# Stick-breaking attention step: ScalarE reads the accumulators, GpSimd adds, and transposes share a PSUM ring with the scores

## The chip, the core and the metric

One core of a Trainium2 chip runs the program. The metric is device time in microseconds (us), the median of several executions. Before the change it is 1325.29 us (three runs, 1322.95 to 1325.57).

## The reference, cut to what matters

One layer is computed for a prompt of 2048 tokens and for 64 tokens of a running stream, in float32:

```
h = rms_norm(x) * g_norm;  z = h @ w_in          # 1024 -> 3072 columns
q_sb, k_sb, v_sb, g_sb, u_pool, g_pool, q_xa, g_xa = split(z)
# A) stick-breaking attention, 8 heads of 64, strictly causal
s = q k^T / 8;  w[q,k] = sigmoid(s[q,k]) * prod_{k<k'<q} sigmoid(-s[q,k']);  o_sb = w v
# B) causal pooling with windows 2/4/8/16;  C) cross-attention into 256 memory tokens
mixed = concat(o_sb * silu(g_sb), o_pool * silu(g_pool), o_xa * silu(g_xa))
y = rms_norm(x + mixed @ w_out) * g_final
```

The change touches the prompt's stick-breaking attention and the output rows (`x + mixed @ w_out` and the last norm) that run beside it. The kernel writes the attention with running products: c[q,k] is the product of sigmoid(-s) from key k to the query, and o = v + sum over k of c[q,k] * (v[k-1] - v[k]). So a score needs one sigmoid and one multiplying scan, and `dv` holds the differences of the values. A projection in near-float32 precision is three matmuls of rounded parts (high x high, high x low, low x high).

## The kernel before, in words

Until about 700 us the kernel normalises x, projects it (L441 to L443), does pooling, cross-attention and the running stream's 64 tokens, and stores queries, keys, values and gates to DRAM. Then comes the attention of the prompt, in four blocks of 512 queries (`s`), each for four pairs of heads (`p`). For each of these, blocks of 512 keys run from the diagonal (`j == s`) down to 0. This is `Stream.attention`, and each key block is two half blocks, one call of `Stream.step` each: 80 steps, and three more that empty the pipe.

The engines' instructions run in the order written (a manual schedule), so the text of `Stream.step` is the order of each engine's queue:

- `score` (L198): 12 matmuls for two query tiles of 128, six into each of two double banks of PSUM (`z`, a ring of two).
- `weigh`: ScalarE turns a double bank into sigmoid(-z) in SBUF (L207), and VectorE runs two scans over it (L212 on the diagonal, L214 elsewhere). A scan below the diagonal starts from the last column of the scan of the key block before it.
- `turn`, three steps later: 16 transposes of 64x128 pieces (fewer on the diagonal) of one block of 128 keys into two single banks (`pt`, a ring of two, L227), which ScalarE copies to SBUF in two copies (L230). A step turns two key blocks; the second `turn` stands behind the two `score` calls of the step.
- `run`: pieces of other dense work fill TensorE, first the gates' projections, then the output rows, three matmuls each (L1119). How many per step is set by `rate`.
- `gather` (L241): the turned weights times `dv` into the single bank `av`. After the last key block of a pair of heads, VectorE adds `vt` to `av` (L252), GpSimd multiplies with the gate (L258) and stores the result to DRAM.

`Rows` is a tile of 128 output rows. `split` rounds the loaded `mixed` on ScalarE (L1098) and takes the rest on GpSimd (L1099). `piece` accumulates eight k-tiles for each half of 512 columns in one bank `acc`; after the eighth VectorE adds x (L1122) and sums squares (L1123). `finish` does the norm on VectorE (L1131 to L1135) and stores on GpSimd's queue. A half is always followed by a stop (`None`), so the next one starts in a later step. There is one bank `av` and one `acc`: who reads them sets when TensorE can write again. Twelve such tiles run beside the attention; the last four run behind it (`tail`), in the double banks `z`.

Of the kernel before, what the change touches and what calls it, by code (L numbers as in the profile page):

```python
# [8 lines left out]
F32 = mybir.dt.float32  # L9
# [4 lines left out]
ALU = mybir.AluOpType  # L14
AX = mybir.AxisListType
PSUM = bass.MemoryType.PSUM
DRAM = bass.MemoryType.DRAM

P = 128
# [5 lines left out]
KT = D // P  # L25
# [9 lines left out]
LO, HI = slice(0, 64), slice(64, P)  # L35
# [8 lines left out]
def tile_hybrid_step(  # L44
# [30 lines left out]
    V, A, G, PE = nc.vector, nc.scalar, nc.gpsimd, nc.tensor  # L75
# [20 lines left out]
    ident = edge[:, 384:]  # L96
# [79 lines left out]
    class Block:  # L176


        def __init__(self, a, j):
            self.a, self.j = a, j  # L180
            p, room = a["p"], a["room"]
            self.K = room("K").rearrange("p (a t) -> p a t", a=2)
            dma(f(self.K), k_d[p][:, j])
            self.V = f(room("V")).rearrange("p (b d) -> p b d", b=4)
            dma(self.V, dv_d[p][:, j])
            self.diag = j == a["s"]
            self.later, a["c"] = a["c"], [None] * 4
# [29 lines left out]
        def turn(self, kb):  # L217


            room = self.a["room"]  # L220
            i0 = kb if self.diag else 0
            pts = [room("pt").rearrange("p (h i q) -> p h i q", h=2, i=4) for _ in range(2)]
            for h in range(2):
                for i in range(i0, 4):
                    for rows, pt in zip((LO, HI), pts):
                        c = self.cs[i][rows, h, kb * P : kb * P + P]
                        PE.transpose(pt[:, h, i], c, ident[rows, rows])  # L227
            w = room("w").rearrange("p (h i q) -> p h i q", h=2, i=4)
            for rows, pt in zip((LO, HI), pts):
                A.copy(w[:, :, i0:, rows], pt[:, :, i0:])  # L230
            turned = w.rearrange("p h i q -> p h (i q)")
            return kb, i0, turned

        def gather(self, kb, i0, turned):

            a, j = self.a, self.j
            room, p, s = a["room"], a["p"], a["s"]
            if self.diag and kb == 0:
                a["av"] = room("av")
            for h, rows in enumerate((LO, HI)):  # L240
                PE.matmul(  # L241
                    a["av"][rows, i0 * P :], self.V[:, kb, rows], turned[:, h, i0 * P :],
                    start=(self.diag and kb == 0), stop=(j == 0 and kb == 3),
                )
            if j == 0 and kb == 0:
                cols = slice(512 * s, 512 * s + 512)
                a["vt"], a["sg"] = room("vt"), room("sg")
                dma(a["vt"], vt_d[p][:, cols])
                dma(a["sg"], sg_d[p][:, cols])
            if j == 0 and kb == 3:  # L250
                o = room("o")
                V.tensor_tensor(o, a["av"], a["vt"], ALU.add)  # L252
                if (s, p) == LAST:

                    V.tensor_tensor(o, o, a["sg"], ALU.mult)
                    last_mixed.append(o)
                else:
                    G.tensor_tensor(o, o, a["sg"], ALU.mult)  # L258
                    store(mix_d[s][:, p], o)

    class Stream:
# [3 lines left out]


        def __init__(self, more):
            self.halves, self.pieces, self.credit = [], [], 0.0
            self.rate, self.more = 0.0, more

        def step(self, block, g):
            t = len(self.halves)
            self.halves.append((block, g))
            self.credit += self.rate
            turned = []
            b, old = self.halves[t - TURN] if t >= TURN else (None, 0)
            if b is not None:
                turned.append(b.turn(2 * old))
            if block is not None:
                first, second = block.score(2 * g), block.score(2 * g + 1)  # L280
                first()
            if b is not None:
                turned.append(b.turn(2 * old + 1))
            if block is not None:
                second()
                if g == 1:
                    block.cs = block.a["c"]
            self.run(self.credit)
            for what in turned:
                b.gather(*what)  # L290
            self.credit = min(self.credit, 6.0)

        def run(self, n):

# [61 lines left out]
    hpool = ctx.enter_context(tc.tile_pool(name="hpool", bufs=1))  # L356
    wpool = ctx.enter_context(tc.tile_pool(name="wpool", bufs=2))
    ps_acc = ctx.enter_context(tc.tile_pool(name="ps_acc", bufs=2, space=PSUM))
    ps_t = ctx.enter_context(tc.tile_pool(name="ps_t", bufs=2, space=PSUM))
    last_scope = ctx.enter_context(ExitStack())  # L360
    ps_x = last_scope.enter_context(tc.tile_pool(name="ps_x", bufs=1, space=PSUM))
    ps_last = last_scope.enter_context(tc.tile_pool(name="ps_last", bufs=1, space=PSUM))

# [271 lines left out]
    for p in range(2):  # L635
        w = chunk_of(GX0 + p)
# [12 lines left out]
    for c in range(2):  # L649
        for j in range(2):  # L650
            w, rows = WINDOWS[2 * c + j], slice(64 * j, 64 * j + 64)
# [65 lines left out]
    for c in range(2):  # L717
        w = chunk_of(U0 + c)
# [15 lines left out]
        w = chunk_of(GP0 + c)  # L734
# [95 lines left out]
    for make, c0 in ((keys, K0), (values, V0)):  # L830
        for p in range(4):
            w = chunk_of(c0 + p)
# [130 lines left out]
    for p in range(4):  # L963
        w = chunk_of(Q0 + p)
# [30 lines left out]
    def cut(t, at, *sizes):  # L995
# [9 lines left out]
    ps_z = ctx.enter_context(tc.tile_pool(name="ps_z", bufs=1, space=PSUM))  # L1005
# [9 lines left out]
        "o": cut(l3, 4096, 512) + cut(ends, 0, 512),  # L1015
        "vt": cut(ends, 512, 512, 512),
        "sg": cut(ends, 1536, 512, 512),
        "z": [ps_z.tile([P, 2, 512], F32, name=f"z{i}") for i in range(2)],
        "av": [ps_acc.tile([P, 512], F32, tag="acc", name="av")],
        "acc": [ps_acc.tile([P, 512], F32, tag="acc", name="acc2")],  # L1020
    })

    def room(name):
        if name == "pt":
            return ps_t.tile([P, 512], F32, tag="pt", name="pt")
        rings[name].append(rings[name].pop(0))
        return rings[name][-1]


    wo = {}  # L1030
# [17 lines left out]
    class Rows:  # L1048
# [56 lines left out]
        def piece(self, half, c):  # L1105
            n, xt = self.n, self.xt
            cols = slice(512 * half, 512 * half + 512)
            if c == 0 and done and half == 0:
                self.z = room("z")
            if c == 0 and not done:  # L1110
                self.acc = room("acc")
            k = self.ks[c]
            out, mh, ml = self.z[:, half] if done else self.acc, self.mh[:, k], self.ml[:, k]
            wh, wl = wo_part(k, "h")[:, cols], wo_part(k, "l")[:, cols]
            passes = [(out, mh, wh), (out, ml, wh)][: 2 if n == P else 1] + [(out[:n], mh[:, :n], wl)]
            if c == 7:
                passes.reverse()
            for i, (o, m, w) in enumerate(passes):
                PE.matmul(o, m, w, start=(c == i == 0), stop=(c == 7 and i == len(passes) - 1))  # L1119
            if c == 7:  # L1120
                for i in range(0, P, n):
                    V.tensor_tensor(xt[:n, cols], out[i : i + n], xt[:n, cols], ALU.add)  # L1122
                V.scalar_tensor_tensor(  # L1123
                    wo["sq"][:n, cols], xt[:n, cols], 1.0, xt[:n, cols], ALU.mult, ALU.mult,
                    accum_out=self.total[:n, half : half + 1],
                )

        def finish(self):
            n, xt = self.n, self.xt
# [18 lines left out]
    def output_rows():  # L1148

        if len(settled) >= SETTLED:  # L1150
            follow()
        if not following:
            return []

        if not done and len(stream.halves) - following[0].born < 2:
            return []
        rows = following.pop()
        while rows.parts:
            rows.split()
        pieces = []  # L1160
        for half in range(2):
            for c in range(KT):

                def piece(half=half, c=c):
                    rows.piece(half, c)
                    i = KT * half + c
                    if i == 1:
                        follow()
                    elif i > 3 and (i - 1) % 3 == 0 and following:
                        following[0].split()  # L1170
                    if i == 15:
                        rows.finish()

                pieces.append(piece)
                if c == KT - 1 and not done:
                    pieces.append(None)
        return pieces

    ready, done = [], False
# [17 lines left out]
    stream, tail = Stream(more), []  # L1197
# [29 lines left out]
            tail[0].split()  # L1227
    while stream.pieces or ready or following:
        stream.piece()
    tail[0].split_late()  # L1230
    tail.append(Rows(T // P - 3, ("K", "K")))


    done = True
# [3 lines left out]
            for c in range(KT - 1):  # L1238
                rows.piece(half, c)

    def rest_of(rows):
        for half in range(2):
            rows.piece(half, KT - 1)
        rows.finish()

    for half in range(2):
        for c in range(KT - 1):
# [4 lines left out]
    prepared(T // P - 2, "K", "K")  # L1252
    tail[2].split_late()
    most(tail[1])
    rest_of(tail[0])
    rest_of(tail[1])
    prepared(T // P - 1, "q", "q")
    tail[3].split_late()
    for rows in tail[2:]:
# [34 lines left out]
```

## Time and profile before

| | before |
|---|---|
| median of 3 runs | 1325.29 us |
| profiled execution: its time, its span | 1323.47 us, 1321.7 us |
| mean granted TensorE clock | 0.981 of 2.4 GHz |
| TensorE matmuls busy (PE) | 1236.6 us, 94% |
| VectorE (DVE) | 799.7 us, 61% |
| ScalarE (ACT) | 520.5 us, 39% |
| GpSimd (POOL) | 338.6 us, 26% |

The profile is one execution. Busy times are shares of the whole span, over stages with different limits; the attention runs from about 700 to 1258 us, the last four row tiles from there to the end. PE is the matmul side of TensorE, PEld its weight loads, SP the queue that starts most DMAs. A row of the waits names the waiting engine and line, then who released it.

### The profile page before, as it was taken

The page shows a single profiled execution, that of the slowest core. Times are in us where ns is not written, and L with a number is a line of the kernel's source. Part 1 is how long each engine was busy: PE and PEld are TensorE (multiplying, and loading weights), DVE is VectorE, ACT ScalarE, POOL GpSimd, SP SyncE. Part 2 cuts the span into 40 slices and gives each one's busy share as a digit, 9 for nine tenths or more (in the row PEclk, how much of TensorE's full clock was granted, in tenths as well). Part 3 has the DMA queues.
Part 4 walks back from the last instruction along what each step waited for, and adds up shares of the span by engine and source line. Part 5 has one row for each costly group of instructions (what it writes and reads, how often), then busy time and mean ns, then how long its engine had stood idle before and what let it go on. Part 6 is the DMA issues. An engine that isn't in the chain of part 4 may idle for free.

```text
span 1321.7 us, 22014 instructions
## 1 busy us (share of the span) xinstructions
PE 1236.6 (94%) x8506; PEld 954.7 (72%) x8506; DVE 799.7 (61%) x1388; ACT 520.5 (39%) x1077; POOL 338.6 (26%) x415
## 2 busy tenths in 40 slices
PE   5899999999999999999999988999988998999987
PEld 5788888688888888887887755666655655666565
DVE  7863445455554442333224596779987787899644
ACT  5641111144444442231013464446445465576510
POOL 3211237234444442222001113321312002012110
PEclk9999999999999999999999999989999998999999
DMA  7534432555555543443256774434443243431221
GB/s 243 189 121 151 150 132 82 172 177 194 172 167 160 171 143 125 146 131 107 87 182 212 286 269 135 154 104 147 134 136 116 101 127 120 136 112 51 93 74 49
DMA packets 115637, 190.30 MB, mean 144 GB/s; under 512 B 9458, under 2 KB 73548, under 8 KB 115532
## 3 DMA queue, kind: packets, MB, share of 16 engines
q1 hardware_dynamic: 95436, 120.95, 29.9%
q0 software_dynamic: 20096, 67.94, 14.2%
q8 instruction: 67, 1.10, 0.4%
q14 instruction: 38, 0.31, 0.1%
HBM read 118.83 MB, written 70.02 MB: 143 GB/s over the span
## 4 chain that ended last, share of the span: by engine, by line
PE 59%; DVE 10%; issue 7%; ACT 4%; POOL 3%; DMA 3%; DVEq 0%; ACTq 0%; SPq 0%; POOLq 0%
PE acc L1119 11%; PE acc L441 8%; PE acc L443 7%; PE acc L442 7%; PE av L241 7%; DVE at_hl L214 5%; PE pt L227 5%; PE z L198 4%; PE z L1119 3%; ACT more_w L230 2%; ACT at_hl L207 1%; POOL psum_w L669 1%; PE pt_p L787 1%; PE pt_r L477 1%; DVE xo L1122 1%
## 5 line engine op out<-in xcount | busy, mean ns | idle before, releaser
L441 PE MATMUL acc<-hh,wh 128*128 128x512 f32 (+2 forms) x960 | 358.3, 374 | 6.5 <-DVE sg L543 5.5
L442 PE MATMUL acc<-hl,wh 128*128 128x512 f32 (+2 forms) x960 | 341.9, 356 | 0.0
L443 PE MATMUL acc<-hh,wl 128*128 128x512 f32 (+2 forms) x960 | 339.9, 355 | 0.0
L230 ACT COPY more_w<-pt 128x512 f32<-128x512 f32 (+3 forms) x320 | 152.0, 528 | 216.6 <-PE pt L227 214.7
L214 DVE TENSOR_TENSOR_SCAN at_hl<-at_hl,at_hl 128x512 f32<-128x512 f32 x148 | 195.1, 1375 | 25.3 <-ACT at_hl L207 25.3
L441 PEld LDWEIGHTS acc<-hh,wh 128*128 128x128 f32 x960 | 182.0, 190 | 32.4 <-DVE sg L543 8.1
L443 PEld LDWEIGHTS acc<-hh,wl 128*128 128x128 f32 x960 | 181.7, 189 | 24.5 <-issue 1.0
L442 PEld LDWEIGHTS acc<-hl,wh 128*128 128x128 f32 x960 | 182.5, 190 | 21.1 <-issue 4.0
L241 PE MATMUL av<-more_w,at_hh 128*64 128x512 f32 (+3 forms) x640 | 140.0, 551 | 11.3 <-DVE ends L252 8.6
L227 PEld LDWEIGHTS pt<-edge,at_hl 64*128 64x128 f32 x1936 | 87.9, 139 | 60.6 <-issue 44.8
L207 ACT ACTIVATE at_hl<-z 128x1024 f32<-128x1024 f32 (+3 forms) x143 | 130.8, 916 | 0.6
L212 DVE TENSOR_TENSOR_SCAN at_hl<-at_hl,edge 128x128 f32<-128x128 f32 (+3 forms) x116 | 92.8, 852 | 34.4 <-ACT at_hl L207 34.4
L1119 PE MATMUL acc<-at_hh,mh 128*128 128x512 f32 x208 | 92.0, 442 | 19.2 <-DVE xo L1122 14.4
L227 PE MATMUL pt<-edge,at_hl 64*128 64x64 f32 x1936 | 102.3, 228 | 5.5 <-ACT more_w L230 3.7
L1099 POOL TENSOR_TENSOR ml<-m,mh 128x256 fp32r<-128x256 f32 (+1 forms) x52 | 58.9, 1144 | 169.2 <-ACT mh L1098 169.0
L241 PEld LDWEIGHTS av<-more_w,at_hh 128*64 128x64 f32 x640 | 37.9, 137 | 79.3 <-issue 48.1
L1119 PE MATMUL acc<-at_hl,mh 128*128 128x512 f32 (+1 forms) x208 | 84.3, 418 | 0.0
L1119 PE MATMUL acc<-at_hh,ml 128*128 128x512 f32 x192 | 79.5, 414 | 1.0 <-POOL ml L1099 1.0
L198 PE MATMUL z<-at_hh 64*128 64x512 f32 (+2 forms) x576 | 70.2, 375 | 0.0
L432 DVE CAST wh<-wr 128x1024 fp32r<-128x1024 f32 x32 | 23.6, 736 | 70.5 <-PE acc L442 34.2
L1119 PEld LDWEIGHTS acc<-at_hh,mh 128*128 128x128 f32 x208 | 41.8, 201 | 32.5 <-DVE xo L1122 15.7
L543 DVE TENSOR_TENSOR sg<-acc,sg 128x512 f32<-128x512 f32 x24 | 16.5, 690 | 69.9 <-ACT sg L542 69.9
(275 smaller groups left out, 1808.0 us busy)
## 6 DMA issues: line engine op xcount, KB each, us to landing
at_hh<-k_d SPq DMA_DIRECT2D x40, 512.0 KB, 5.3
wr<-in_w_in_dram SPq DMA_DIRECT2D x24, 512.0 KB, 4.7
at_hh<-dv_d SPq DMA_DIRECT2D x40, 256.0 KB, 3.5
xt_x<-in_x_prompt_dram SPq DMA_DIRECT2D x16, 512.0 KB, 4.0
xq<-qx_d SPq DMA_DIRECT2D x64, 128.0 KB, 4.0
k_d<-k POOLq DMA_DIRECT2D x16, 512.0 KB, 3.8
out_dram<-rt POOLq DMA_DIRECT2D x32, 256.0 KB, 3.5
q_d<-q POOLq DMA_DIRECT2D x16, 512.0 KB, 2.9
```

The source lines that it names most:

```text
L198: PE.matmul(z[:, h, :w], a["q"][rows, part, at], K[rows, keys, :w], start=(part == keys == 0), stop=(part == 1),)
L207: A.activation(c[:, :, :n], z[:, :, :n], AF.Sigmoid, scale=-1.0)
L212: V.tensor_tensor_scan(cc, cc, edge[:, 512 - n :][:, ::-1], 0.0, ALU.mult, ALU.max)
L214: V.tensor_tensor_scan(cc, cc, cc, self.later[i][:, h, 0:1], ALU.mult, ALU.bypass)
L227: PE.transpose(pt[:, h, i], c, ident[rows, rows])
L230: A.copy(w[:, :, i0:, rows], pt[:, :, i0:])
L241: PE.matmul(a["av"][rows, i0 * P :], self.V[:, kb, rows], turned[:, h, i0 * P :], start=(self.diag and kb == 0), stop=(j == 0 and kb == 3),)
L441: PE.matmul(out, wh[:, k], hi, start=(k == 0), stop=False)
L442: PE.matmul(out, wh[:, k], lo, start=False, stop=False)
L443: PE.matmul(out, wl[:, k], hi, start=False, stop=(k == KT - 1))
L1099: engine.tensor_tensor(ml, m, f(mh), ALU.subtract)
L1119: PE.matmul(o, m, w, start=(c == i == 0), stop=(c == 7 and i == len(passes) - 1))
```

## The change

- The transposes of a key block go into one double bank, one half of the rows in each bank, taken from the ring `z`, which now has three double banks; the two single banks `pt` are gone. Off the diagonal one ScalarE copy reads both banks.
- A step does its two `turn` calls first, then the two `score` calls.
- The result of a pair of heads: ScalarE copies `av` to SBUF, GpSimd adds `vt` (the last pair of the last block keeps VectorE).
- The output rows beside the attention: ScalarE copies `acc` to SBUF, GpSimd adds x; the sum of squares and `finish` are put in a list `due` and issued in the next step, behind its scores.
- In the tail, the last pieces of the first two row tiles come before the `finish` of either.

```diff
 def turn(self, kb):
-            pts = [room("pt").rearrange("p (h i q) -> p h i q", h=2, i=4) for _ in range(2)]
+            pt = room("z").rearrange("p r (h i q) -> p r h i q", h=2, i=4)
             for h in range(2):
                 for i in range(i0, 4):
-                    for rows, pt in zip((LO, HI), pts):
+                    for r, rows in enumerate((LO, HI)):
                         c = self.cs[i][rows, h, kb * P : kb * P + P]
-                        PE.transpose(pt[:, h, i], c, ident[rows, rows])
+                        PE.transpose(pt[:, r, h, i], c, ident[rows, rows])
             w = room("w").rearrange("p (h i q) -> p h i q", h=2, i=4)
-            for rows, pt in zip((LO, HI), pts):
-                A.copy(w[:, :, i0:, rows], pt[:, :, i0:])
+            if i0:
+                for r, rows in enumerate((LO, HI)):
+                    A.copy(w[:, :, i0:, rows], pt[:, r, :, i0:])
+            else:
+                A.copy(
+                    w.rearrange("p h i (r q) -> p r (h i) q", r=2), pt.rearrange("p r h i q -> p r (h i) q")
+                )
 def gather(self, kb, i0, turned):
                 o = room("o")
-                V.tensor_tensor(o, a["av"], a["vt"], ALU.add)
                 if (s, p) == LAST:
+                    V.tensor_tensor(o, a["av"], a["vt"], ALU.add)
                     V.tensor_tensor(o, o, a["sg"], ALU.mult)
                 else:
+                    A.copy(o, a["av"])
+                    G.tensor_tensor(o, o, a["vt"], ALU.add)
                     G.tensor_tensor(o, o, a["sg"], ALU.mult)
 def step(self, block, g):
             if b is not None:
-                turned.append(b.turn(2 * old))
+                turned = [b.turn(2 * old + k) for k in range(2)]
             if block is not None:
-                first, second = block.score(2 * g), block.score(2 * g + 1)
-                first()
-            if b is not None:
-                turned.append(b.turn(2 * old + 1))
-            if block is not None:
-                second()
+                for k in range(2):
+                    block.score(2 * g + k)()
                 if g == 1:
                     block.cs = block.a["c"]
+            self.settle()
             self.run(self.credit)
+        def settle(self):
+            while self.due:
+                self.due.pop(0)()
-        "z": [ps_z.tile([P, 2, 512], F32, name=f"z{i}") for i in range(2)],
+        "z": [ps_z.tile([P, 2, 512], F32, name=f"z{i}") for i in range(3)],
 def piece(self, half, c):      # of Rows
             if c == 7:
-                for i in range(0, P, n):
-                    V.tensor_tensor(xt[:n, cols], out[i : i + n], xt[:n, cols], ALU.add)
-                V.scalar_tensor_tensor(... square, summed into self.total ...)
+                if n == P and not done:
+                    A.copy(wo["sq"][:, cols], out)
+                    G.tensor_tensor(xt[:, cols], wo["sq"][:, cols], xt[:, cols], ALU.add)
+                    stream.due.append(lambda: self.square(half))
+                else:
+                    for i in range(0, P, n):
+                        V.tensor_tensor(xt[:n, cols], out[i : i + n], xt[:n, cols], ALU.add)
+                    self.square(half)
 def output_rows():
                     if i == 15:
-                        rows.finish()
+                        stream.due.append(rows.finish)
-    def rest_of(rows):
-        for half in range(2):
-            rows.piece(half, KT - 1)
-        rows.finish()
+    def rest_of(*tiles):
+        for rows in tiles:
+            for half in range(2):
+                rows.piece(half, KT - 1)
+        for rows in tiles:
+            rows.finish()
-    rest_of(tail[0])
-    rest_of(tail[1])
+    rest_of(*tail[:2])
```

## Rows read from the trace of the kernel before

**Rows 1.** Busy time by stretch: span, PE, PEld, DVE, ACT, POOL, clock, DMA.

```profile
755.00:800.00 45.00, 36.89 (x398) 23.34 (x397) 40.88 (x41) 30.53 (x59) 10.85 (x9) 0.95 0.79 277
800.00:1050.00 250.00, 231.70 (x1904) 154.54 (x1903) 200.35 (x305) 120.57 (x224) 59.75 (x54) 0.96 0.40 125
1050.00:1258.00 208.00, 196.57 (x1799) 124.38 (x1798) 170.29 (x213) 122.02 (x212) 32.05 (x32) 0.98 0.35 108
```

**Rows 2.** Waits, 686 to 1258 us: engine, line, releaser: total, times, longest.

```profile
PE acc L1119 <- DVE xo L1122: 14.4, 9, 3.5
PE av L241 <- DVE ends L252: 8.6, 3, 4.1
PE acc L1119 <- ACT mh L1098: 4.8, 2, 2.4
PE pt L227 <- ACT more_w L230: 4.6, 14, 0.7
PE pt L227 <- DVE at_hl L214: 1.8, 3, 0.7
PE av L241 <- ACT more_w L230: 1.5, 8, 0.2
```

**Rows 3.** Busy time by stretch, around drops of the granted clock.

```profile
860.00:867.40 7.40, 6.13 (x14) 4.79 (x15) 3.73 (x8) 0.00 (x0) 1.15 (x1) 0.54 0.21 75
924.80:928.90 4.10, 4.03 (x11) 2.69 (x12) 4.04 (x6) 0.76 (x3) 2.25 (x2) 0.59 0.41 126
1287.20:1290.80 3.60, 3.46 (x8) 2.78 (x9) 2.46 (x8) 0.11 (x1) 0.00 (x0) 0.53 0.30 115
```

**Rows 4.** Timeline of one full step: start, duration, engine, line, tile.

```profile
1220.20 0.71 PE L227 MATMUL pt<-edge,at_hl 64*128 64x64 f32 x16
1220.73 1.64 PE L198 MATMUL z<-at_hh,at_hh 64*128 64x512 f32 x12
1221.01 1.08 ACT L230 COPY more_w<-pt 128x512 f32<-128x512 f32 x2 [1.32 <-PE pt L227]
1221.96 1.05 ACT L207 ACTIVATE at_hl<-z 128x1024 f32<-128x1024 f32 x1
1222.20 0.67 PE L227 MATMUL pt<-edge,at_hl 64*128 64x64 f32 x16
1222.80 0.50 PE L1119 MATMUL acc<-at_hh,mh 128*128 128x512 f32 x1
1224.38 1.94 PE L241 MATMUL av<-more_w,at_hh 128*64 128x512 f32 x8
```

**Rows 5.** Timeline: second transposes of a step whose scores lie on the diagonal.

```profile
1143.45 0.71 PE L227 MATMUL pt<-edge,at_hl 64*128 64x64 f32 x15 [0.22 <-ACT more_w L230]
```

**Rows 6.** Timeline: an accumulator is read and written again; scans beside GpSimd.

```profile
1163.64 0.66 DVE L1122 TENSOR_TENSOR xo<-acc,xo 128x512 f32<-128x512 f32 x1
...
1164.36 0.50 PE L1119 MATMUL acc<-at_hh,mh 128*128 128x512 f32 x1 [0.85 <-DVE xo L1122]
...
1164.69 0.39 PE L1119 MATMUL acc<-at_hh,ml 128*128 128x512 f32 x1
...
1165.56 3.42 DVE L214 TENSOR_TENSOR_SCAN more_c<-more_c,at_hl 128x512 f32<-128x512 f32 x2
...
1165.72 2.18 POOL L258 TENSOR_TENSOR ends<-ends 128x512 f32<-128x512 f32 x1 [4.26 <-DVE ends L252]
```

**Rows 7.** Timeline of VectorE: the scans of a full step, nothing on GpSimd.

```profile
1079.08 4.81 DVE L214 TENSOR_TENSOR_SCAN at_hl<-at_hl,at_hl 128x512 f32<-128x512 f32 x4 [1.92 <-ACT at_hl L207]
```

**Rows 8.** Source line L258 on GpSimd: shortest, median, longest ns.

```profile
L258 POOL TENSOR_TENSOR at_hl<-at_hl,ends x8: 1271/2074/2192, 726.3 to 1212.2; 128x512 f32<-128x512 f32 x8
```

**Rows 9.** Timeline behind the attention: VectorE and TensorE, first two row tiles.

```profile
1283.85 0.08 DVE L1123 DVE_READ_ACCUMULATOR sq<-xo 128x1 f32 x1
...
1286.60 0.68 DVE L1122 TENSOR_TENSOR at_hl<-z,at_hl 128x512 f32<-128x512 f32 x1
...
1287.34 0.80 PE L1119 MATMUL z<-at_hl,at_hh 128*128 128x512 f32 x1 [4.18 <-DVE at_hl L1122]
```

More of the change, by code (lines that the diff above doesn't have):

```diff
@@ L267, in __init__ @@
         def __init__(self, more):
-            self.halves, self.pieces, self.credit = [], [], 0.0
+            self.halves, self.pieces, self.credit, self.due = [], [], 0.0, []
             self.rate, self.more = 0.0, more
@@ L358, in tile_hybrid_step @@
     ps_acc = ctx.enter_context(tc.tile_pool(name="ps_acc", bufs=2, space=PSUM))
-    ps_t = ctx.enter_context(tc.tile_pool(name="ps_t", bufs=2, space=PSUM))
     last_scope = ctx.enter_context(ExitStack())
+    ps_t = last_scope.enter_context(tc.tile_pool(name="ps_t", bufs=2, space=PSUM))
     ps_x = last_scope.enter_context(tc.tile_pool(name="ps_x", bufs=1, space=PSUM))
@@ L1023, in room @@
     def room(name):
-        if name == "pt":
-            return ps_t.tile([P, 512], F32, tag="pt", name="pt")
         rings[name].append(rings[name].pop(0))
@@ L1120, in piece, with square @@
             if c == 7:
-                for i in range(0, P, n):
-                    V.tensor_tensor(xt[:n, cols], out[i : i + n], xt[:n, cols], ALU.add)
[L1123 to L1126, printed above, removed]
+                if n == P and not done:
[6 more added lines that the diff above has]
+                    self.square(half)
+        def square(self, half):
+            n, cols = self.n, slice(512 * half, 512 * half + 512)
+            V.scalar_tensor_tensor(
+                wo["sq"][:n, cols], self.xt[:n, cols], 1.0, self.xt[:n, cols], ALU.mult, ALU.mult,
+                accum_out=self.total[:n, half : half + 1],
+            )
         def finish(self):
@@ L1229, in tile_hybrid_step @@
         stream.piece()
+    stream.settle()
     tail[0].split_late()
```

## The prediction

> **What bounds the kernel now.** I read the busy time by stretch first. In the stretches from 800 to 1258 us, where nearly all that the change touches lies, TensorE is busy 231.7 + 196.6 = 428.3 of 458 us (94%), VectorE 370.6 (81%), ScalarE 242.6, GpSimd 91.8 [rows 1]. So TensorE sets the pace there, with some 30 us of holes. From 755 to 800 us it is the other way round: VectorE 40.9 of 45, TensorE 36.9. Then the waits of TensorE, to see what the holes are: 14.4 us for VectorE to read the row accumulator `acc`, 8.6 for it to read `av`, 4.8 for ScalarE's casts of `mixed`, 4.6 + 1.5 for ScalarE's copies of the transposes, and only 1.8 for scans that are late [rows 2]. The reader is to see that the two largest are not waits for long work: the read itself takes 0.66 us [rows 6], but it stands in VectorE's queue behind scans. Last the clock: the long waits come with stretches at the lower of the two levels, 1.2 instead of 2.4 GHz, visible as a mean of 0.54 to 0.59 over a few us [rows 3].
>
> **What goes.** (1) `acc` and `av`: ScalarE has time to read them, being half idle, and nothing long stands ahead of its copies: the step's last sigmoid is issued some us before the last piece. In a step TensorE then has the gathers (1.94 us), transposes and scores to do before it needs `acc` again [rows 4], and a copy of 512 columns is about half of the 1.08 us that two take. So 14.4 + 8.6 = 23.0 us go. I let 3 come back, for the `av` waits before 800 us: there VectorE is the fuller engine, and the next transposes would wait for scans instead. That leaves 20.0. The 4.8 us for casts stay, as the change does not touch them. (2) The copies of both key blocks are now issued early, so the gathers find them done: 1.5 us. (3) The clock: 7.4 x 0.46 = 3.4 us are lost in the stretch at 860, 4.1 x 0.41 = 1.7 in that at 924.8; three more like the second stand at 973, 1024 and 1065, each just behind a wait that goes. That is 10.2; part of it is the hole itself, so I take 8 (bounds 0 and 10.2). (4) The tail: the second tile's first half is added at 1286.60, behind the first tile's `finish`, and TensorE starts at 1287.34, when it has been read [rows 9]. With the new order the add follows the square that ends at 1283.93; with 0.68 of its own and the 0.06 that the same step takes at 1287.28 to 1287.34, TensorE starts at about 1284.7: 2.6 us. The stretch behind it ran at 0.53, 3.6 x 0.47 = 1.7 us [rows 3], which should go with the hole. Together 4.3.
>
> Sum: 20.0 + 1.5 + 8 + 4.3 = 33.8 us.
>
> **What comes.** (5) The ring of three. A step takes four double banks: transposes A, transposes B, scores 1, scores 2. So scores 2 always gets the bank of transposes A, and waits for their copy. In the step of rows 4, transposes take 1220.73 - 1220.20 = 0.53 us to issue and scores 1222.20 - 1220.73 = 1.47, half of it for one. Scores 2 could thus start at 1220.20 + 0.53 + 0.53 + 0.74 = 1222.00. The copy starts at 1221.01; no row has a copy of 1024 columns, so I bound it by one copy and by both, 0.54 and 1.08, and take the 1.05 of the sigmoid of 1024 columns: done at 1222.06, seen by TensorE 0.06 later. A wait of 0.12, after which the first matmul costs 0.1 more (0.33 to the next one instead of the usual 0.23 [rows 6]; I count half, as weights are loaded ahead). To this comes a changed boundary: row pieces started 0.07 before the end of the transposes [rows 4] and will start about at the end of the scores, +0.05. Some 0.2 us for each of the 4 x (1+2+3) x 2 = 48 steps below the diagonal: 9.6 us (bounds 2.4, if the copy hides wholly, and 17, if ScalarE comes 0.15 later on average). In the 32 diagonal steps scores are short, and the wait is longer; but there the second transposes now wait for the same copies (0.22 at one place, [rows 5], and 4.6 in all [rows 2]): I count no difference, and no gain from the 4.6. The other uses of the ring are covered: scores 1 takes the bank of the previous scores 2, whose sigmoid is over before the gathers end.
>
> (6) Merging two copies into one saves ScalarE 0.03 us of 1.08: nothing, as its time is not the limit. ScalarE gets 15 copies of `av` and 24 of `acc` (12 tiles, two halves), 39 x 0.54 = 21 us in 458 with over 200 free. The copy of `av` stands ahead of the next step's copy of transposes: the gathers end at 1226.32, the copy at about 1226.9, and that next copy starts 0.81 behind its transposes, at about 1227.0. It just fits: 0, with 15 x 0.25 = 4 as the other end.
>
> (7) Scans. The first sigmoid of a step now stands behind the second transposes' copy as well. That copy can run at 1222.06 to 1223.1, so the sigmoid starts at 1223.1 and not 1221.96: scans that start when it arrives, as those of [rows 7] do, end 1.1 us later. Transposes need the scans of two steps before in every second step. That slack is mostly several us (only 1.8 us are waited now), but it is short where a diagonal block leaves short steps, and it shrinks by what steps (1) and (3) take from the steps.
>
> (8) VectorE loses 24 + 15 adds of 0.66 us, 26 us. GpSimd gets 39 adds that read two tensors in SBUF, and beside such an operation a pair of scans takes 3.42 us [rows 6] against 4.81 / 2 = 2.41 [rows 7]: 1.0 us each, 39 us. So VectorE gets 13 us more, not less: 384 of about 440 us, 87%. GpSimd itself, 39 x 2.07 = 81 us more [rows 8], stays far from full. Its queue now has adds behind `store`s that wait for a `finish`, but the square that needs an add comes a step later, behind 4.8 us of scans.
>
> The Trainium skill says on this (SBUF — State Buffer, "Who interferes with whom") that a VectorE instruction with two SBUF inputs and a GpSimd instruction that reads SBUF take the same port as a lock, and the later one is blocked until the other is over. The old adds had one input in PSUM and were outside this; the scans have two in SBUF. The trace agrees: the pair grew by 1.0 us beside one GpSimd operation of 2.18.
>
> For (7) and (8) together I take 8 us: about five places behind diagonals at 1.1, and three places late in the attention at 0.8. Bounds: 0, if the slack holds, and 44, if each of 40 second steps waits the full 1.1. The row nearest to it is the 1.8 us of [rows 2], so I stay near the lower end.
>
> Net: 33.8 - 9.6 - 8 = 16.2 us. The profiled execution took 1323.47 us (span 1321.7), and so 1307.3; the median of the runs is 1.8 above it, and so 1309.
>
> **Rivals.** *Everything hides.* Scores 2 and scans have slack, and the clock stays up: 23.0 + 1.5 + 10.2 + 4.3 - 2.4 = 36.6, 1289. For it: 1.8 us of waits for scans. Against: VectorE is at 81% already.
>
> *The waits change their name.* TensorE gets to the transposes earlier and waits there for the scans that delayed the reads of `acc` before; (1) and (3) come back, 4.3 + 1.5 of gains stand against 9.6: 1329. With some of (1) kept it is no change, 1323 to 1329. For it: before 800 us it is so. Against: beyond that, reads were late by their place in the queue, and the queue had slack.
>
> *The scans become the bound (slower).* Scans are later by 1.1 us and blocked by GpSimd, and in every second step TensorE stands before the transposes. It decides from (33.8 - 9.6) / 40 = 0.6 us per second step; at 1.1 us the sum is 44 + 9.6 - 33.8 = 20 slower, 1345. For it: 3.42 against 2.41. Against: that happens in 39 of 160 pairs of scans, and steps with two pieces last some 6 us, against 4.81 of scans.
>
> *ScalarE is late too.* Its queue holds the casts too, for which TensorE waits 4.8 us already; if half of the waits for `acc` stay, 1317. This lies in the forecast's own range.
>
> **How the numbers follow.** Forecast 0.58 (1298 to 1320, from the bounds of (3), (5) and (7)), everything hides 0.15, change of name 0.14, scans the bound 0.13. A measurement of this kernel tells 0.2%, 2.7 us, from no change. Faster: 0.58 + 0.15 + 0.03 of the third case = 0.76; same 0.10; slower 0.14. The range goes from 1288 to 1331: it leaves out most of the last case and the best end of the second.
>
> **What would show it.** The waits of TensorE for L1122 and L252 gone, and in their place short waits of the scores for L230, 0.1 to 0.3 us in some 50 steps; fewer stretches at the lower clock level (those with a cast's wait stay); the gap at 1287 shorter by 2.6 us; VectorE's busy time no lower despite 39 adds fewer. Wrong: waits of the transposes for scans above 25 us, or `acc` still waited for, now for ScalarE or GpSimd.

## Result and profile after the change

| | before | after |
|---|---|---|
| median (range) of 4 runs each, side by side | 1324.12 us (1322.71 to 1325.57) | 1307.40 us (1305.97 to 1309.45) |
| profiled execution: time, span | 1323.47, 1321.7 us | 1305.97, 1304.3 us |
| mean granted TensorE clock | 0.981 | 0.985 |

The ratio is 0.9877, with a 95% interval of 0.9859 to 0.9894: 16.7 us less. First the engines' busy time, from the page of after (busy us, share of the span, instructions).

```profile
PE 1234.1 (95%) x8506; PEld 929.8 (71%) x8506; DVE 804.4 (62%) x1349; ACT 529.9 (41%) x1004; POOL 406.5 (31%) x454
```

VectorE has 39 instructions fewer (1349, from 1388) and is busier than before, 804.4 us against 799.7. GpSimd rises by 68 us. TensorE does the same work. By stretch (columns as in [rows 1]), on after:

```profile
755.00:800.00 45.00, 37.07 (x396) 21.82 (x392) 37.56 (x38) 30.39 (x50) 11.79 (x9) 0.89 0.76 267
800.00:1050.00 250.00, 238.57 (x1963) 148.87 (x1965) 207.46 (x289) 131.87 (x206) 98.23 (x76) 0.97 0.42 131
1050.00:1241.00 191.00, 187.41 (x1730) 109.56 (x1727) 170.00 (x197) 118.15 (x165) 54.52 (x43) 0.98 0.36 111
```

The attention's last gather now ends at 1244.5 instead of 1257.4, and TensorE's idle time between 800 us and that end falls from 29.7 us [rows 1] to 11.4 + 3.6 = 15.0 (between 1241 and 1244.5 it is never idle). At first the change loses time: the attention's first scores start at 685.1 (686.2 before), but the step with the first output rows ends at 811.2 (807.0 before). All of the gain lies behind that step. The waits of TensorE in after, 680 to 1260 us, answer to [rows 2]:

```profile
PE z L227 <- DVE at_hl L214: 7.9, 7, 2.1
PE acc L1126 <- DVE xo L1135: 6.8, 2, 4.9
PE acc L1126 <- ACT mh L1105: 3.5, 2, 2.1
PE z L198 <- ACT more_w L233: 2.9, 12, 0.3
PE z L198 <- ACT more_w L231: 1.9, 7, 0.3
```

The wait for `av` (8.6) is gone. For `acc` 14.4 became 6.8, in two places only: the two halves of the output-row tile of the running stream (64 rows), which had 3.8 of the 14.4 (1.84 and 1.95). Its reads were left on VectorE, since the new branch asks for `n == P`. The timeline of after shows the four scans ahead of one of them, which took 5.25 us before, and then the read:

```profile
920.11 7.20 DVE L214 TENSOR_TENSOR_SCAN at_hl<-at_hl,at_hl 128x512 f32<-128x512 f32 x4
...
927.23 1.38 DVE L1135 TENSOR_TENSOR xo<-acc,xo 64x512 f32<-64x512 f32 x2
...
928.67 0.80 PE L1126 MATMUL acc<-at_hh,mh 128*128 128x512 f32 x1 [4.88 <-DVE xo L1135]
```

What is new is 7.9 us of transposes that wait for scans (1.8 before) and 4.8 of scores that wait for the copies of transposes. Three quarters of the former lie ahead of 800 us; the waits of after from 755 to 800:

```profile
PE z L227 <- DVE at_hl L214: 5.9, 5, 2.1
```

A full step of after answers to [rows 4]:

```profile
1211.13 1.21 PE L227 MATMUL z<-edge,at_hl 64*128 64x64 f32 x32
...
1212.15 0.94 PE L198 MATMUL z<-at_hh,at_hh 64*128 64x512 f32 x6
1212.22 1.93 ACT L233 COPY more_w<-z 128x1024 f32<-128x1024 f32 x2 [1.97 <-PE z L227]
...
1213.29 0.96 PE L198 MATMUL z<-at_hh,at_hh 64*128 64x512 f32 x6 [0.20 <-ACT more_w L233]
...
1214.03 1.96 ACT L207 ACTIVATE at_hl<-z 128x1024 f32<-128x1024 f32 x2
...
1214.18 0.50 PE L1126 MATMUL acc<-at_hh,mh 128*128 128x512 f32 x1
```

The second scores wait 0.20 us for the first copy. From the first transpose to the first row piece pass 3.05 us here, 2.60 in [rows 4]; by the median of the 22 steps that have full scores, full transposes and pieces it is 0.19 more. The step shown is longer than most: its first copy starts 1.09 us behind the first transpose, in nearly all others 0.81. In those the second scores start 0.31 us behind the last of the first, instead of 0.23, and 0.05 behind the end of the copy, and the next pair of them follows after 0.34 instead of 0.23. Both sigmoids come after both copies, the first of them 2.90 us after the step's start, against 1.76 in [rows 4].

Around the drops of the clock, on after (columns as in [rows 1]):

```profile
772.00:780.00 8.00, 6.26 (x46) 3.94 (x46) 6.57 (x10) 3.70 (x4) 0.00 (x0) 0.57 0.55 171
796.00:807.00 11.00, 9.45 (x45) 6.74 (x42) 6.50 (x8) 4.87 (x8) 4.74 (x4) 0.53 0.28 93
926.00:933.00 7.00, 4.33 (x10) 2.93 (x11) 6.93 (x9) 0.00 (x0) 2.24 (x4) 0.51 0.97 307
1093.00:1100.50 7.50, 6.62 (x15) 4.90 (x16) 7.50 (x5) 1.65 (x5) 5.63 (x4) 0.54 0.34 126
1271.00:1275.00 4.00, 3.21 (x14) 2.66 (x15) 3.37 (x12) 0.30 (x1) 0.00 (x0) 1.00 0.00 0
```

There are four stretches at 1.2 GHz in the attention instead of eight, but longer ones: 30.7 us in all, 34.1 before. In them one row matmul follows the other after 0.43 us, elsewhere after 0.23, so about half of such a stretch is lost where TensorE is busy. Up to 807 us they grew from 6.8 to 17.1 us, behind it they shrank from 27.3 to 13.7. The second row's stretch starts at 796.5, behind transposes that waited for scans:

```profile
794.57 0.46 PE L227 MATMUL z<-edge,at_hl 64*128 64x64 f32 x8 [1.98 <-DVE at_hl L214]
795.75 0.78 PE L227 MATMUL z<-edge,at_hl 64*128 64x64 f32 x18 [0.72 <-DVE at_hl L214]
```

The last row is the tail, now at full clock ([rows 3] has 0.53 there). Its hole is 1.81 us, which was 4.56 (a hole is counted here from the start of the last matmul before it to that of the first behind it; of it 1.43 are idle, and 4.18 were in [rows 9]):

```profile
1271.05 0.69 DVE L1135 TENSOR_TENSOR at_hl<-z,at_hl 128x512 f32<-128x512 f32 x1
...
1271.79 0.50 PE L1126 MATMUL z<-at_hl,at_hh 128*128 128x512 f32 x1 [1.43 <-DVE at_hl L1135]
```

One gain was not in the forecast. In the last three steps there are no scores, so the second transposes followed the first at once and stood before two full `pt` banks. Before:

```profile
1245.23 0.71 PE L227 MATMUL pt<-edge,at_hl 64*128 64x64 f32 x16
1246.67 0.27 PE L227 MATMUL pt<-edge,at_hl 64*128 64x64 f32 x1 [0.73 <-ACT more_w L230]
1247.16 0.71 PE L227 MATMUL pt<-edge,at_hl 64*128 64x64 f32 x15 [0.22 <-ACT more_w L230]
1247.80 0.50 PE L1119 MATMUL acc<-at_hl,mh 128*128 128x512 f32 x1
```

After, with three double banks:

```profile
1235.14 1.35 PE L227 MATMUL z<-edge,at_hl 64*128 64x64 f32 x32
1236.42 0.50 PE L1126 MATMUL acc<-at_hl,mh 128*128 128x512 f32 x1
```

2.57 us became 1.28. The three steps gain 1.4, 1.3 and 1.4 us, 4.1 together.

### The profile page after: what moved, and what is told of

Its sections match the earlier page's. It is cut to its first block, busy times and chain, and to the rows that moved or that the text cites. A ratio compares the mean times of both kernels' runs of the same rounds, so it can differ in the third digit from the quotient of the medians.

```text
span 1304.3 us, 21910 instructions
## 1 busy us (share of the span) xinstructions
PE 1234.1 (95%) x8506; PEld 929.8 (71%) x8506; DVE 804.4 (62%) x1349; ACT 529.9 (41%) x1004; POOL 406.5 (31%) x454
## 3 DMA queue, kind: packets, MB, share of 16 engines
q0 software_dynamic: 20096, 67.94, 14.4%
## 4 chain that ended last, share of the span: by engine, by line
PE 62%; DVE 7%; issue 6%; ACT 3%; POOL 3%; DMA 2%; DVEq 0%; ACTq 0%; SPq 0%; POOLq 0%
PE acc L1126 11%; PE av L246 8%; PE acc L450 8%; PE acc L452 8%; PE acc L451 7%; PE z L198 6%; PE z L227 4%; PE z L1126 3%; DVE at_hl L214 3%; ACT more_w L233 2%; POOL psum_w L678 1%; PE pt_p L796 1%; PE pt_r L486 1%; DMA sg_d<-sg 1%; DVE at_hl L212 1%
## 5 line engine op out<-in xcount | busy, mean ns | idle before, releaser
L214 DVE TENSOR_TENSOR_SCAN at_hl<-at_hl,at_hl 128x512 f32<-128x512 f32 x148 | 209.1, 1471 | 41.2 <-ACT at_hl L207 41.2
L233 ACT COPY more_w<-z 128x1024 f32<-128x1024 f32 x112 | 108.8, 1017 | 132.1 <-PE z L227 130.8
L246 PE MATMUL av<-more_w,at_hh 128*64 128x512 f32 (+3 forms) x640 | 135.2, 544 | 0.0
L207 ACT ACTIVATE at_hl<-z 128x1024 f32<-128x1024 f32 (+3 forms) x143 | 123.7, 919 | 1.1 <-PE z L198 0.5
L212 DVE TENSOR_TENSOR_SCAN at_hl<-at_hl,edge 128x128 f32<-128x128 f32 (+3 forms) x116 | 97.6, 901 | 23.8 <-ACT at_hl L207 23.8
L227 PEld LDWEIGHTS z<-edge,at_hl 64*128 64x128 f32 x1936 | 73.7, 140 | 52.5 <-issue 32.6
L1106 POOL TENSOR_TENSOR ml<-m,mh 128x256 fp32r<-128x256 f32 (+1 forms) x52 | 66.3, 1284 | 99.5 <-ACT mh L1105 99.4
L227 PE MATMUL z<-edge,at_hl 64*128 64x64 f32 x1936 | 85.1, 228 | 7.9 <-DVE at_hl L214 7.9
L198 PE MATMUL z<-at_hh 64*128 64x512 f32 (+2 forms) x576 | 81.5, 396 | 3.8 <-ACT more_w L233 1.7
L1131 POOL TENSOR_TENSOR xo<-sq,xo 128x512 f32<-128x512 f32 x24 | 39.9, 1661 | 80.2 <-ACT sq L1130 80.1
```

Source lines behind the costliest of these rows:

```text
L198: PE.matmul(z[:, h, :w], a["q"][rows, part, at], K[rows, keys, :w], start=(part == keys == 0), stop=(part == 1),)
L207: A.activation(c[:, :, :n], z[:, :, :n], AF.Sigmoid, scale=-1.0)
L212: V.tensor_tensor_scan(cc, cc, edge[:, 512 - n :][:, ::-1], 0.0, ALU.mult, ALU.max)
L214: V.tensor_tensor_scan(cc, cc, cc, self.later[i][:, h, 0:1], ALU.mult, ALU.bypass)
L227: PE.transpose(pt[:, r, h, i], c, ident[rows, rows])
L233: A.copy(w.rearrange("p h i (r q) -> p r (h i) q", r=2), pt.rearrange("p r h i q -> p r (h i) q"))
```

## The experiments

All were timed in five rounds beside the kernel before (medians 1321.18 for the first four, 1324.0 for the next four, 1323.73 for the last three).

| run | what | median us | ratio to before [95%] | clock |
|---|---|---|---|---|
| e1_reads | only the reads on ScalarE, adds on GpSimd, squares and `finish` a step later | 1309.54 | 0.9910 [0.9887, 0.9933] | 0.983 |
| e2_ring | only the ring of three, transposes first | 1337.38 | 1.0121 [1.0099, 1.0143] | 0.977 |
| e3_tail | only the tail's order | 1316.37 | 0.9965 [0.9952, 0.9978] | 0.983 |
| e4_mid | after, scores 1 between the transposes | 1304.58 | 0.9865 [0.9842, 0.9887] | 0.984 |
| e5_sample | after, 64-row tile read by ScalarE too | 1302.08 | 0.9835 [0.9821, 0.9848] | 0.988 |
| e6_vadd | after, adds on VectorE a step later | 1302.49 | 0.9843 [0.9824, 0.9863] | 0.990 |
| e7_reads_tail | after without the ring | 1306.51 | 0.9858 [0.9840, 0.9876] | 0.983 |
| e8_best | e7 and 64-row tile | 1299.90 | 0.9818 [0.9803, 0.9832] | 0.985 |
| e9_vbest | e8 and adds on VectorE | 1286.81 | 0.9724 [0.9706, 0.9741] | 0.990 |
| e10_last | e9 and a free bank in the last three steps | 1283.41 | 0.9703 [0.9684, 0.9721] | 0.989 |
| e11_ringv | e9 with the ring of three | 1292.34 | 0.9772 [0.9755, 0.9790] | 0.993 |

**Reads alone (e1_reads).** The kernel before with this part of the change only:

```diff
-                V.tensor_tensor(o, a["av"], a["vt"], ALU.add)
+                    A.copy(o, a["av"])
+                    G.tensor_tensor(o, o, a["vt"], ALU.add)
...
+                    A.copy(wo["sq"][:, cols], out)
+                    G.tensor_tensor(xt[:, cols], wo["sq"][:, cols], xt[:, cols], ALU.add)
+                    stream.due.append(lambda: self.square(half))
```

> The kernel before with one part of the change alone: ScalarE copies av and acc, GpSimd adds, squares and finish are issued a step later. Transposes keep their two single banks and their places (A, scores 1, scores 2, B), the tail its order. Theory (the gain is the reads that leave VectorE's queue, the ring and the new order of a step cost): this part alone is at least as fast as the whole change less its tail, 1300 to 1310 us, and the waits of the transposes for scans are below the 7.9 us that the whole change has. Rival (the gain is the new order of the step, and the reads come back as waits for scans): 1316 to 1324 us.

Measured: 0.9910. Its first waits of TensorE, 680 to 1262 us:

```profile
PE pt L227 <- DVE at_hl L214: 7.7, 8, 2.1
PE acc L1127 <- DVE xo L1136: 7.2, 2, 5.1
PE acc L1127 <- ACT mh L1106: 4.9, 2, 2.4
```

Most of the gain is in this part. The waits for scans are already what they are in after (7.7 against 7.9, and 5.5 against 5.9 ahead of 800 us), so they come with the moved reads and adds, not with the ring and its later sigmoid. No run defers the squares and `finish` alone, so their share in this part stays open.

**Ring alone (e2_ring).** The diff of `turn`, of `step` and of the banks, without the rest.

```diff
-            pts = [room("pt").rearrange("p (h i q) -> p h i q", h=2, i=4) for _ in range(2)]
+            pt = room("z").rearrange("p r (h i q) -> p r h i q", h=2, i=4)
...
+                turned = [b.turn(2 * old + k) for k in range(2)]
```

> The kernel before with the other part alone: transposes and scores share three double banks, both transposes first; VectorE reads av and acc as before, the tail keeps its order. Theory: slower than before, 1326 to 1340 us: 0.18 us in each step with pieces, sigmoids 0.9 us later, so reads behind scans are later too; against that 4 us from the last three steps, whose second transposes no longer wait for copies. Rival (the order is the gain): 1308 to 1318 us.

Measured: 16.2 us slower, 1.0121. Its waits, 680 to 1260 us:

```profile
PE acc L1118 <- DVE xo L1121: 16.0, 9, 3.2
PE av L246 <- DVE ends L257: 9.1, 3, 4.4
PE z L227 <- DVE at_hl L214: 4.0, 4, 1.8
```

By the medians of their kinds the steps cost 9.3 together, and the last three give 4.2 back. With the reads still on VectorE, their waits grow (16.0 + 9.1, from 23.0, so 2.1), those for scans by 2.2, and the clock falls from 0.981 to 0.977: 0.023 x 1335.0 = 30.7 us against 0.019 x 1321.7 = 25.1, 5.6 more. That is 15.0; the two profiled executions lie 13.3 us apart, the medians 16.2, so it is a rough sum. The theory's range held.

**Tail alone (e3_tail).**

```diff
+    def rest_of(*tiles):
+        for rows in tiles:
+            for half in range(2):
+                rows.piece(half, KT - 1)
+        for rows in tiles:
+            rows.finish()
```

> The kernel before with the tail's order alone: the last pieces of the first two row tiles before either finish. Theory: 2.6 us of wait and 1.7 us of half clock go, 1319 to 1321 us. Rival (the wait moves to the third tile's bank, as the ring still has two): 1323 to 1325 us.

Measured: 0.9965, 4.8 us; the hole in the tail goes from 4.56 to 1.82 us and the stretch at 1.2 GHz behind it is gone. By the trace the tail is 4.4 us shorter. Its attention, whose code is that of before, is 3.0 us shorter too: a stretch of 6.8 us at 1.2 GHz near 1103 us did not come. So much can differ between two executions. The three parts alone make -0.90% + 1.21% - 0.35% = -0.04%, the whole -1.23%. They don't add: the ring costs much less where the reads have left VectorE.

**Later sigmoid (e4_mid).** After, in the order transposes A, scores 1, transposes B, scores 2:

```diff
+            for k in range(2):
+                if b is not None:
+                    turned.append(b.turn(2 * old + k))
+                if block is not None:
...
```

> The whole change, but the step in the order transposes A, scores 1, transposes B, scores 2, still from the ring of three. The first sigmoid then stands behind one copy and not two. Theory (the waits of transposes for scans, 7.9 us on the page and three holes of 1.3 to 4.7 us near 773, 794 and 891 us, come from sigmoids that are 0.9 us later): those waits fall by half or more, 1299 to 1304 us. Rival (they come from GpSimd's adds that block scans): the waits stay, 1305 to 1310 us.

Measured: 0.9865, its interval over that of after. The waits for scans fell from 7.9 to 5.7 only, where the theory of the later sigmoid had them fall by half or more. With e1_reads this leaves little of term (7).

**The 64-row tile (e5_sample).** After, with its two pieces of PSUM copied by ScalarE (the second into a spare tile `stage`) and added by GpSimd:

```diff
+                elif not done:
+                    A.copy(wo["sq"][:n, cols], out[:n])
+                    A.copy(self.stage[:n, cols], out[n:])
+                    G.tensor_tensor(xt[:n, cols], wo["sq"][:n, cols], xt[:n, cols], ALU.add)
+                    G.tensor_tensor(xt[:n, cols], self.stage[:n, cols], xt[:n, cols], ALU.add)
```

> The whole change, and the 64-row tile of the running stream too: ScalarE copies both halves of acc to SBUF, GpSimd adds them, the square comes a step later. Theory (the 6.8 us that TensorE still waits for VectorE to read acc are this tile's two halves, for which the change kept the old path, and they bring 6.8 us of half clock near 926 us): those waits go to under 1 us, the stretch at half clock goes, ratio to before 0.979 to 0.983 (the whole change has 0.9877). Rival (VectorE is full there, and the transposes wait for scans instead): 0.986 to 0.989.

Measured: 0.9835, 5.3 us under after, the intervals apart, a little short of the theory's range. The wait of 6.8 is gone, and a part came back in the queue of transposes (e5_sample's waits, 680 to 1260 us):

```profile
PE z L227 <- DVE at_hl L214: 10.5, 10, 2.1
PE z L198 <- ACT more_w L233: 4.1, 13, 1.0
```

**Who adds (e6_vadd).** After, with the copies on ScalarE as they are, and the adds on VectorE, from SBUF, in the next step (`due`):

```diff
-                    G.tensor_tensor(xt[:, cols], wo["sq"][:, cols], xt[:, cols], ALU.add)
-                    stream.due.append(lambda: self.square(half))
+                    def added():
+                        V.tensor_tensor(xt[:, cols], wo["sq"][:, cols], xt[:, cols], ALU.add)
+                        self.square(half)
+                    stream.due.append(added)
```

> The whole change, with the adds of vt and x on VectorE, from the SBUF copies, a step later, behind the scores' scans; GpSimd keeps only the gate's product. Theory (an add on GpSimd costs VectorE's scans 1.0 us by blocking them, one on VectorE 0.66): VectorE's busy time falls by some 5 to 13 us from 804, TensorE's waits for scans fall from 7.9 to 4 to 6 us, ratio 0.984 to 0.988. Rival (moving the adds to GpSimd is worth its 39 x 0.66 = 26 us on VectorE): VectorE's busy time rises, waits for scans over 10 us, ratio 0.990 to 1.000.

Measured: 0.9843, 4.9 us under after (the intervals just touch). The largest group of scans in after, 680 to 1250 us, and GpSimd's adds (busy, mean ns, then idle time before):

```profile
L214 DVE TENSOR_TENSOR_SCAN at_hl<-at_hl,at_hl 128x512 f32<-128x512 f32 x148 | 209.1, 1471 | 41.2 <-ACT at_hl L207 41.2
```

```profile
L1131 POOL TENSOR_TENSOR xo<-sq,xo 128x512 f32<-128x512 f32 x24 | 39.9, 1661 | 80.2 <-ACT sq L1130 80.1
```

The same scans in e6_vadd, and the add that VectorE does instead:

```profile
L214 DVE TENSOR_TENSOR_SCAN at_hl<-at_hl,at_hl 128x512 f32<-128x512 f32 x148 | 190.9, 1346 | 44.9 <-ACT at_hl L207 44.9
...
L1137 DVE TENSOR_TENSOR xo<-sq,xo 128x512 f32<-128x512 f32 x24 | 17.2, 718 | 5.7 <-ACT sq L1134 5.7
```

The five groups of scans in this view take 356.8 us instead of 378.8: 22 us for 39 adds (24 of `x`, 15 of `vt`), 0.56 each. VectorE's other instructions take some 7 us less too, and its own adds 27 us (0.67 to 0.72 each). So its busy time is about the same (802.8 against 804.4), where the theory had it fall by 5 to 13; the waits for scans fall from 7.9 to 4.1, as the theory said.

**Without the ring (e7_reads_tail, e8_best).** e7 is the diffs of e1 and e3 together, on the old banks and in the old order; e8 adds that of e5.

> The whole change without its ring: two single banks for transposes, two double banks for scores, the old order of the step; reads and tail as in the change. Theory (the ring costs 0.18 us in 58 steps with pieces and gives back 0.2 in steps without and 1.3 in each of the last three, some 3 us net): ratio 0.984 to 0.988, the same as or a little better than the whole change's 0.9877. Rival (reads and ring need each other, as each alone gave less than the whole): 0.990 or more.

> As the one without the ring, and the 64-row tile too is copied by ScalarE and added by GpSimd. Theory: both gains add up, ratio 0.977 to 0.982, faster than the whole change and than each alone. Rival: waits for scans take the place of the tile's reads, 0.984 to 0.988.

Measured: 0.9858 and 0.9818. Both lie a little below their counterparts with the ring (0.9877 and 0.9835), the intervals overlapping: on top of the moved reads the ring brings nothing. Both theories' ranges held, but in e8 the waits for scans grow to 10.1, as its rival said.

**The best of each (e9_vbest, e11_ringv).** e8 with the edit of e6 for all three kinds of adds; and the same with the ring.

```diff
-                    G.tensor_tensor(xt[:n, cols], wo["sq"][:n, cols], xt[:n, cols], ALU.add)
-                    G.tensor_tensor(xt[:n, cols], self.stage[:n, cols], xt[:n, cols], ALU.add)
-                    stream.due.append(lambda: self.square(half))
+                    def both():
+                        V.tensor_tensor(xt[:n, cols], wo["sq"][:n, cols], xt[:n, cols], ALU.add)
+                        V.tensor_tensor(xt[:n, cols], self.stage[:n, cols], xt[:n, cols], ALU.add)
+                        self.square(half)
+                    stream.due.append(both)
```

> Reads by ScalarE for all row tiles and results, adds on VectorE from SBUF a step later, the tail's new order, transposes in their two single banks in the old order. Theory (what helps is that TensorE no longer waits for reads behind scans; GpSimd's adds only cost): ratio 0.976 to 0.980, below the 0.9818 of the same with GpSimd adding, waits of the transposes for scans 4 to 7 us instead of 10.1. Rival (adds on VectorE pay only with the ring): 0.981 to 0.984.

> The whole change (ring of three, transposes first) with the 64-row tile read by ScalarE too and all adds on VectorE a step later. Theory: the ring costs the same 0.1 to 0.3% here as without, against its gain in the last three steps, ratio 0.977 to 0.981. Rival (VectorE lighter, the ring's later sigmoids no longer matter): 0.974 to 0.976.

Measured: 0.9724, better than the theory's range, and 0.9772, in it. Here the ring costs 5.5 us, the intervals apart. The waits in e9_vbest, 680 to 1260 us:

```profile
PE pt L227 <- ACT more_w L230: 6.1, 19, 0.7
PE acc L1133 <- ACT mh L1112: 4.8, 2, 2.4
PE pt L227 <- DVE at_hl L214: 2.6, 3, 1.9
```

Against e8 the waits for scans go from 10.1 to 2.6 us (behind 800 us from 4.8 to nothing) and the clock from 0.985 to 0.990; the span is 11.9 us shorter. The stretch that holds most of the reads now has 2.3 us of idle TensorE in 250 and the full clock:

```profile
800.00:1050.00 250.00, 247.67 (x2139) 164.70 (x2138) 223.44 (x325) 149.69 (x276) 68.08 (x56) 1.00 0.44 139
```

**A free bank at the end (e10_last).** e9, with the second transposes of the last three steps in a double bank of the idle score ring:

```diff
+            banks = room("z") if spare else None
+            pts = [(banks[:, r] if spare else room("pt")).rearrange("p (h i q) -> p h i q", h=2, i=4) for r in range(2)]
...
+                turned.append(b.turn(2 * old + 1, block is None))
```

> As the one before, but in the last three steps, which have no scores, the second transposes take a free double bank of the scores. Theory: the three holes of 0.95 to 1.2 us near 1220 to 1240 us, where the second transposes wait for the first one's copies, go: 2.8 to 4 us less, 0.974 to 0.978. Rival (the row tile behind them is late in any case): no difference.

Measured: 0.9703, median 3.4 us under e9, the span 4.6, the intervals just overlapping: the saving that the theory gave, though the ratio lies below its range. The waits of transposes for copies fall from 6.1 to 2.1:

```profile
PE pt L228 <- ACT more_w L231: 2.1, 10, 0.2
```

So the one useful thing in the ring, a free bank where there are no scores, is to be had without it. This kernel, 1283.41 us, is the fastest of all.

## Why the prediction was right, point by point

The forecast was 1309 us and the time is 1307.4. The mechanism was right: TensorE stood behind reads of 0.66 us that were late by their place in VectorE's queue, and they went when ScalarE took them (e1_reads). The terms were less right than their sum.

- **(1) Reads, 23.0 less 3 that come back ahead of 800 us: this is the term that was mis-sized most.** 23.0 us of waits became 6.8; with a third row for `av`, 0.9 us, that is 17.1 less. What stayed is the 64-row tile, whose branch I had not followed in the diff, and its waits grew from 3.8 to 6.8; e5_sample shows that they can go. And what came back ahead of 800 us is more than 3: the waits for scans grew from 0.7 to 5.9, by 5.2. So the term is 11.9, not 20.0. That VectorE is the fuller engine there is not all of it: with the adds back on VectorE, 3.5 (e6_vadd) and 2.6 us (e9_vbest) are left of the 5.9.
- **(2) Gathers waiting for copies, 1.5:** gone.
- **(3) Clock, 8: less than half came.** Of the stretches that were to go, those at 860, 973, 1024 and 1065 went; that at 924.8 is the 64-row tile's and became longer. Together they went from 20.5 to 6.8 us, at half clock 6.8 us saved, near the 8. What I put at nothing is the clock that new waits cost: ahead of 807 us the stretches grew by 10.2 us, 5.1 at half clock, next to late scans (773.3, 794.6). That leaves 1.7, or 3.9 if the time in which TensorE waits in these stretches is not counted. That is about as much as two executions of one code can differ by (e3_tail). In e6 and e9, with fewer late scans, the attention has 17.1 and 10.2 us at 1.2 GHz, instead of 30.7.
- **(4) Tail, 4.3:** measured 4.56 - 1.81 = 2.75 of hole and 1.7 of clock, 4.4; alone 4.8 of the median (e3_tail).
- **(5) Ring, 0.2 for each of 48 steps, 9.6.** The 36 of them with row pieces got 0.18 longer by the median (6.4 us), at the second scores, which stand behind the first copy, as worked out; most of these delays are too short to be listed as waits, and the view of the waits has 19. Of the other twelve the five with full transposes got 0.23 shorter: their gathers no longer wait 0.20, which (2) counts. Of the 20 diagonal steps with pieces, counted at nothing, most cost 0.18 to 0.37, and six, whose second transposes waited for copies before, got 0.13 to 0.40 shorter. Together about 7 us, the 1.5 of (2) included, where the forecast has 9.6 - 1.5 = 8.1. The copy of 1024 columns takes 1.02 us by its mean (1.05 was taken). What failed is "no gain from the 4.6" of [rows 2]: the last three steps gain 4.1.
- **(6) ScalarE, 0:** no wait of TensorE for the copies of `acc` or `av` is left.
- **(7) and (8) Scans, 8.** Behind 800 us, where this was meant, the waits for scans went from 1.1 to 2.0: 0.9. The slack held, near the lower bound. The later sigmoid hardly matters (e1_reads). The GpSimd adds slow the scans by 0.56 us each, not 1.0, and VectorE's busy time rises by 5 us, not 13. The Trainium skill (SBUF — State Buffer, "Who interferes with whom") says that a VectorE instruction with two SBUF inputs contends with a GpSimd instruction that reads SBUF. The trace agrees: of the 192 scans of L214 in after, the 102 that run beside no tensor operation of GpSimd take 1.29 us at most, and the 90 that do take 1.69 on the mean.

The sum can be taken from step to step, from the end of one step's gathers to that of the next, in both traces (79 steps). Waits for reads take 17.1 us less, for scans 6.0 more, for the casts of `mixed` and GpSimd's part of them 2.1 less, the clock 3.9 less. What is left, the matmuls and copies that the ring moves, takes 5.1 more, with the gain of 4.1 in the last three steps and the 1.5 of (2) in it. That is 12.0; with 0.8 ahead of these steps and 4.6 in the tail it gives the 17.5 us between the two profiled executions. Against the forecast the reads gave 8.1 us less and the clock 4.1 less. The scans took 7.1 less, and the ring with (2) was 3.0, the casts 2.1 better. So the 16.2 was met by errors that nearly cancel, which is luck. The rival "the waits change their name" holds ahead of 800 us, where the steps up to 811 us lose 5.0, and not behind it. The scans did not become the bound.

Two things stay open. Moving the adds to VectorE brings 0.3% on after (e6_vadd) but 0.9% on e8 (e9_vbest); the waits for scans fall by more there (10.1 to 2.6 us, against 7.9 to 4.1), and the clock is higher in both. From e5_sample to e11_ringv, which have both the ring and the tile, it brings 0.6%, so, as far as the intervals tell, part of the difference goes with the tile and part with the ring; why is open. And VectorE's busy time is the same with its own adds as beside GpSimd's, yet it is in time more often; that the adds now stand at a fixed place in its queue, behind the scores, is an argument and was not shown.

## What to carry to other kernels

Where the fullest engine waits for a short read in the queue of a backlogged engine, give the read to an engine whose queue is short, and look for every branch that reads the same buffer: one small tile left behind kept 6.8 us of waits (3.8 before). Moving the arithmetic behind the read is a separate question: an add on an idle engine that disturbs the busy one can be worse than the same add done a step later by the busy one. Test each part of a joint change alone and on top of the others; the ring cost 16 us alone, 1 to 6 beside the moved reads, and its one gain could be had without it.

## What the runs showed of the hardware

- A GpSimd add of 1.66 us between tensors in SBUF lengthened VectorE's scans by 0.56 us on the mean (22 us over 39 adds), nearly as much as the 0.67 to 0.72 us that the add takes on VectorE itself.
- The length of a hole in TensorE's work does not tell alone whether the clock falls. In before and in e3_tail the same code waits equally long for a cast, 2.42 us until 1103.40 and 2.43 until 1102.65, and only before falls to 1.2 GHz (columns as in [rows 1]). Before:

```profile
1102.50:1110.00 7.50, 6.59 (x15) 4.87 (x16) 4.34 (x3) 1.76 (x5) 4.62 (x4) 0.54 0.04 12
```

e3_tail:

```profile
1102.00:1110.00 8.00, 7.03 (x28) 4.52 (x30) 4.54 (x4) 1.51 (x5) 4.65 (x4) 1.00 0.14 42
```

- One copy of 1024 columns from two banks of PSUM took 1.02 us, two copies of 512 took 1.08 [rows 4].
